# Split float32 products issued for two sums in turn, in a two-block transformer on one core

## The chip, the core and the metric

The kernel runs on one core of one Trainium2 chip. The metric is device microseconds of one execution. The kernel before took a median of 2975.62 us over three runs (2973.6 to 2980.26).

Five engines appear in the profile: PE (TensorE, the matmuls, with PEld for the weight loads that go beside them), DVE (VectorE), ACT (ScalarE), POOL (GpSimd) and SP (SyncE, which here issues nearly all DMAs).

## The reference, cut to what matters

Two different blocks, each of two layers, act on 256 tokens of 1024 features in float32.

```python
def first_block(x, ...):                    # two layers
    for l in range(2):
        mixed = concat(delta_rule_heads, gated_conv, forgetting_attention)   # from x @ w_in[l]
        x = layer_norm(ALPHA * x + (mixed * mix_scale[l]) @ w_out[l])
        y = swiglu(x, ffn_w1, ffn_w3, ffn_w2) if l == 0 else mixture_of_experts(x)   # 8 experts, 2 a token
        x = layer_norm(ALPHA * x + y)

def second_block(x, mem, ...):              # two layers
    for l in range(DEPTH):
        x = x + 0.5 * swiglu_2(rmsnorm(x, ffn1_norm[l]), ...)
        proj = rmsnorm(x, mix_norm[l]) @ w_in[l]
        # window attention, a gated linear recurrence, attention over a memory; each projected to D_MODEL
        merged = g[:, :, 0] * br_attn + g[:, :, 1] * br_lru + g[:, :, 2] * br_mem
        x = x + merged @ w_out[l]
        x = x + 0.5 * swiglu_2(rmsnorm(x, ffn2_norm[l]), ...)
    return rmsnorm(x, final_norm)
```

The sketch of the first block is shortened; the second is close to the reference's own lines. Nearly all arithmetic is in the projections, in the feed-forward layers and in the experts' three matrices (1024 x 3584 each, 8 experts).

## The kernel before, in words

**Split products.** A float32 operand is cut into two parts: `hi`, the value rounded to the type that the matmul takes in one pass (float32r), and `lo`, what is left. A product of two such operands is made of three matmuls into one PSUM sum: hi by hi, hi by the other's lo, lo by the other's hi. `mm3` (line 216) issues these three back to back. Each matmul has a weight load of its own, so that PE and PEld have the same count.

**Weights** come from DRAM as one long stream in the order of their use. `load_chunk` (line 382) issues one DMA on SP's queue for up to 2048 columns into a `raw` buffer. `run_pieces` (line 317) cuts each chunk into tiles of up to 1024 columns: ACT writes `hi` (line 199), DVE subtracts and writes `lo` (line 203). There are four buffers each for `hi` and `lo` (`NHL = 4`). A `hi` buffer comes free when PE has used it.

**projS / projG** (lines 400 to 440): features on partitions. A group of output chunks of 128 features is summed over K chunks; two neighbouring chunks share one PSUM bank of 2 x 256 columns. For each k and each chunk j of the group comes one `mm3`. The weights are the stationary operand, a chunk of 256 tokens the moving one. In a group of two or more chunks every third matmul goes on to another sum; in a group of one chunk all matmuls of the group go to the same sum. Groups of one chunk are: all but the first two chunks of each feed-forward down projection (`ffn`, line 606), the last chunks of `w_out` (line 873, from `MO = 6`) and of `w_out_2` (line 1837, from chunk 4), and all gates and branch projections of the second block's mixer (`gcol`, line 1812, and `merge`, line 1816).

**projMG** (line 448): tokens on partitions; two sums, one for each half of the tokens, in two banks, one `mm3` after the other. The mixers of the first block leave part of their projections unsplit (plain float32); those the change leaves alone.

**Experts** (`_experts`, line 1420). A block of work is one expert `e` and 512 of its 3584 hidden columns `fb`: `up` sums `moe_w1` over eight k into one bank, then `moe_w3` over eight k into another, 24 matmuls of 512 columns each. Then `Silu` of the first (ACT, tile `es`) and its product with the second (DVE, `es`). `down` transposes `es`, splits it into `hh` and `hl`, and advances two sums `py` of 512 features, again three matmuls on the one and three on the other. `down` of a block is issued behind `up` of the next. There are 56 blocks. `finish` brings an expert's two sums back to token order.

**Order of the work.** The kernel's text gives each instruction a place, but a planner sets the final order on each engine: of the instructions whose inputs and buffers it reckons ready, it takes the one that comes first in the text. The engines then keep that order. So an ACT or DVE instruction that waits for PE holds back those put behind it.

**Mixer of the second block.** Gates for `NG = 5` columns of 128 features (three branches each) come first, then for each column `merge(c)`: three branch projections (4, 4 and 8 chunks of K), and behind the first three of these one more column of gates. Tiles `gg` hold at most 18 gates.

Of the kernel before, what the change touches and what calls it, by code (L numbers as in the profile page):

```python
# [15 lines left out]
ALU = mybir.AluOpType  # L16
# [16 lines left out]
# ---------------------------------------------------------------- constants  # L33
# [56 lines left out]
# ------------------------------------------------- small parameters (layout)  # L90
# [76 lines left out]
NG = 5  # L167
# [10 lines left out]
class K:  # L178
# [17 lines left out]
    # ---- engine shorthands  # L196
# [36 lines left out]
    # ---- constants and parameters  # L233
# [12 lines left out]
    def setup(self):  # L246
        """loads of the small arrays; what is worked out from them follows in setup2"""
# [7 lines left out]
    def setup2(self):  # L255
        """one step a call: the parameters, then the constants"""
# [26 lines left out]
    def setup3(self):  # L283
        """what is worked out from them once"""
# [73 lines left out]
    def preload(self, st, pieces, m):  # L358
        """the loads of the first m chunks of what comes next"""
# [31 lines left out]
    # ---- PSUM tiles: one bank each  # L391
# [6 lines left out]
    # ---- projections, features on partitions:  out[col, tok]  # L398
# [4 lines left out]
    def projG(self, st, groups, K_, rhs, evict, korder=None, hook=None, pre=None, pin=False, whole=None):  # L403
        """groups: lists of (name, idx, col0); evict(i, n, ps[128, n, 256]) for chunks i .. i + n - 1; a step for every
        split of weights"""
# [3 lines left out]
        i0, m = 0, 0  # L409
# [35 lines left out]
    # ---- projection, tokens on partitions: out[tok, cols]  # L445
# [4 lines left out]
    def projMG(self, st, name, idx, col0, w, K_, lhs, evict, tag="mm", pin=False, whole=None):  # L450
# [3 lines left out]
        for k in range(K_):  # L454
# [9 lines left out]
            for t in range(2):  # L464
                s = slice(t * 128, t * 128 + 128)
                if whole is not None:
                    self.mm(banks[t][:, :w], whole[:, k, s], rp, k == 0, k == K_ - 1)
                    continue
                self.mm3(banks[t][:, :w], (lh[:, s], ll[:, s]), rp, start=(k == 0), stop=(k == K_ - 1))
# [4 lines left out]
    # ---- norms  # L474
    def stats(self, n, mean, late_=LATE, st=None):
        """sums over the features by token of n chunks: (bank [128, 2, 2], add(c, z[, zq]))"""
# [7 lines left out]
        def add(c, z):  # L484
            """the last two chunks go to the products alone, those before are summed up first"""
# [42 lines left out]
    def ln_finish(self, st, n, eps):  # L528
        """-> PSUM bank [128, 2, 256]: rstd, -mu*rstd on every partition"""
# [16 lines left out]
    def rms_finish(self, st, n=D, out=None):  # L546
        """-> rstd on every partition [128, 256], and by token on partitions [128, 2]"""
# [22 lines left out]
    def xhl(self, k):  # L570
        """the parts of a chunk of the input; the norm's chunks are worked out a little ahead of their use"""
# [8 lines left out]
    # ---- SwiGLU; rms: works out the rstd of the input tokens, where the input doesn't hold it yet  # L580
    def ffn(self, st, n1, n3, n2, idx, evict, rms=None, mid=None, mid2=None):
# [24 lines left out]
        groups = [[(n2, idx, 0), (n2, idx, 128)]] + [[(n2, idx, c * 128)] for c in range(2, KD)]  # L606
        rhs2 = lambda k: (h[:, k], l[:, k])
        if mid2:
            self.projS(st, groups[:-1], KF, rhs2, evict)
            mid2()  # L610
            self.projS(st, groups[-1:], KF, rhs2, lambda i, n, ps: evict(KD - 1, n, ps))
        else:
            self.projS(st, groups, KF, rhs2, evict)

    # ---- block 1: residual, then LN
# [17 lines left out]
    def ln_apply(self, z, b, gname, bname, hl=True, gain=None):  # L633
        """x = LN(z) and its parts; with gain: the parts of gain * x, and the statistics of x for the RMS norm"""
# [1337 lines left out]
```

## Time and profile before

| what | value |
|---|---|
| median of three runs | 2975.62 us (2973.6 to 2980.26) |
| profiled execution: its own span, first to last instruction | 2981.4 us |
| PE busy, share of the span, matmuls | 2920.8 us, 98%, 19525 |
| PEld busy | 2647.2 us, 89% |
| DVE busy | 2159.7 us, 72% |
| ACT busy | 1752.4 us, 59% |
| DMA, mean over the span | 223 GB/s |

The profiled execution has no other time listed than its span; it is 5.8 us over the median of the runs. Stages by time from the start: first block's mixer 0 to 258 us, feed-forward 258 to 424, second mixer 424 to 683, experts 683 to 1672, and then the second block, each of whose two layers has a feed-forward layer, the mixer and another feed-forward layer.

How to read it: a matmul's recorded duration overlaps the next one's, since matmuls are pipelined. The price of a matmul in a stream is therefore the distance from its start to the next one's start, and the busy share of PE does not tell by itself how near it is to its limit. In a row of the timeline the columns are start, duration, engine, line, operation, output and inputs, shape and count; square brackets give the idle time before it and what ended it.

### The profile page before, as it was taken

How to read it: one execution, taken by the hardware profiler on the slowest of the kernel's cores; microseconds unless marked ns; L12 is line 12 of the kernel's file. 1: busy time of each engine (PE TensorE's matmuls, PEld its weight loads, DVE VectorE, ACT ScalarE, POOL GpSimd, SP SyncE). 2: the span in 40 equal slices, each digit the busy share in tenths (PEclk: the TensorE clock that was granted, in tenths of full speed). 3: DMA queues.
4: the chain of work that ended last, by engine and by line, in shares of the span. 5: the costliest groups of instructions: out<-in, count | busy, mean ns of one | idle time of the engine just before them, and what ended most of it. 6: DMA issues, size and time to landing. Idle time of an engine off the chain costs nothing.

```text
span 2981.4 us, 48787 instructions
## 1 busy us (share of the span) xinstructions
PE 2920.8 (98%) x19525; PEld 2647.2 (89%) x19525; DVE 2159.7 (72%) x3156; ACT 1752.4 (59%) x2576; POOL 77.8 (3%) x142
## 2 busy tenths in 40 slices
PE   8999999999999999999999999999999999999998
PEld 7889997888888887788878899989999999999998
DVE  5656566559988897998989866676766665866764
ACT  4345444348787776778777744565554444664543
POOL 0100001000000000000000000100000000100000
PEclk9999999899999999999999999999999999999999
DMA  5225543229899998998999745524555555335552
GB/s 196 99 86 181 187 142 128 84 95 359 346 335 364 358 357 307 350 349 335 359 369 353 281 178 184 177 107 156 206 191 189 181 189 191 137 113 194 196 192 105
DMA packets 104205, 663.77 MB, mean 223 GB/s; under 512 B 11808, under 2 KB 17952, under 8 KB 28576
## 3 DMA queue, kind: packets, MB, share of 16 engines
q1 hardware_dynamic: 101664, 658.46, 59.7%
q8 instruction: 156, 2.56, 0.3%
q10 hardware_dynamic: 2304, 2.10, 0.2%
q14 instruction: 81, 0.66, 0.1%
HBM read 657.36 MB, written 3.15 MB: 222 GB/s over the span
## 4 chain that ended last, share of the span: by engine, by line
PE 57%; DVE 2%; ACT 1%; issue 0%; POOL 0%; POOLq 0%; DVEq 0%; ACTq 0%
PE ps_mm L214 47%; PE py L214 5%; PE ps_fx L214 2%; PE ps_sm L214 2%; DVE lo L203 1%; PE ps_fx L224 0%; PE ps_sm L224 0%; DVE aa L1769 0%; ACT hi L199 0%; DVE gi L203 0%; PE ps_st L214 0%; DVE aa L203 0%; ACT xr L200 0%; DVE y L211 0%; DVE ffab L203 0%
## 5 line engine op out<-in xcount | busy, mean ns | idle before, releaser
L203 DVE TENSOR_TENSOR lo<-raw,hi 128x1024 fp32r<-128x1024 f32 (+2 forms) x1216 | 1434.1, 1205 | 398.7 <-ACT hi L199 385.4
L199 ACT ACTIVATE hi<-raw 128x1024 fp32r<-128x1024 f32 (+2 forms) x1216 | 1246.8, 1044 | 648.8 <-PE ps_mm L214 480.9
L214 PE MATMUL ps_mm<-xh,hi 128*128 128x256 f32 x2736 | 775.7, 284 | 13.0 <-ACT hi L199 8.0
L214 PE MATMUL ps_mm<-xh,lo 128*128 128x256 f32 x2736 | 771.5, 283 | 2.3 <-DVE lo L203 2.3
L214 PE MATMUL ps_mm<-xl,hi 128*128 128x256 f32 x2736 | 771.3, 282 | 0.0
L214 PEld LDWEIGHTS ps_mm<-xh,hi 128*128 128x128 f32 x2736 | 519.4, 190 | 19.0 <-ACT hi L199 8.7
L214 PEld LDWEIGHTS ps_mm<-xh,lo 128*128 128x128 f32 x2736 | 519.1, 190 | 6.4 <-issue 3.3
L214 PEld LDWEIGHTS ps_mm<-xl,hi 128*128 128x128 f32 x2736 | 519.9, 190 | 2.8 <-issue 2.4
L214 PE MATMUL ps_mm<-lo,xgh 128*128 128x512 f32 x896 | 356.7, 398 | 0.7
L214 PE MATMUL ps_mm<-hi,xgl 128*128 128x512 f32 x896 | 350.0, 391 | 0.0
L214 PE MATMUL ps_mm<-hi,xgh 128*128 128x512 f32 x896 | 349.5, 392 | 0.0
L214 PE MATMUL ps_mm<-ffl,hi 128*128 128x256 f32 x880 | 250.2, 284 | 0.0
L214 PE MATMUL ps_mm<-ffh,hi 128*128 128x256 f32 x880 | 250.2, 284 | 0.0
L214 PE MATMUL ps_mm<-ffh,lo 128*128 128x256 f32 x880 | 250.1, 284 | 0.0
L214 PEld LDWEIGHTS ps_mm<-lo,xgh 128*128 128x128 f32 x896 | 168.4, 188 | 48.4 <-DVE lo L203 16.1
L214 PEld LDWEIGHTS ps_mm<-hi,xgh 128*128 128x128 f32 x896 | 168.5, 188 | 35.5 <-ACT hi L199 0.2
L214 PEld LDWEIGHTS ps_mm<-hi,xgl 128*128 128x128 f32 x896 | 168.7, 188 | 32.4
L214 PE MATMUL py<-lo,hh 128*128 128x512 f32 x448 | 178.5, 398 | 0.5
L214 PE MATMUL py<-hi,hl 128*128 128x512 f32 x448 | 174.8, 392 | 0.5
L214 PEld LDWEIGHTS ps_mm<-ffl,hi 128*128 128x128 f32 x880 | 170.1, 193 | 0.0
L214 PEld LDWEIGHTS ps_mm<-ffh,lo 128*128 128x128 f32 x880 | 170.0, 193 | 0.0
L214 PEld LDWEIGHTS ps_mm<-ffh,hi 128*128 128x128 f32 x880 | 170.0, 193 | 0.0
(432 smaller groups left out, 3756.9 us busy)
## 6 DMA issues: line engine op xcount, KB each, us to landing
raw<-in_sm SPq DMA_DIRECT2D x336, 1024.0 KB, 7.0
raw<-in_s SPq DMA_DIRECT2D x248, 1024.0 KB, 4.8
raw<-in_s SPq DMA_DIRECT2D x40, 512.0 KB, 3.3
raw<-in_s SPq DMA_DIRECT2D x32, 256.0 KB, 2.7
raw<-in_mem SPq DMA_DIRECT2D x5, 1024.0 KB, 4.9
kv<-kvt ACTq DMA_DIRECT2D x16, 128.0 KB, 2.3
raw<-kv SPq DMA_DIRECT2D x16, 128.0 KB, 2.7
raw<-in_s SPq DMA_DIRECT2D x2, 1005.0 KB, 6.8
```

Source lines behind the costliest of these rows:

```text
L199: return self.nc.scalar.activation(out, in_, func, scale=scale, **kw)
L203: return self.nc.vector.tensor_tensor(out=out, in0=a, in1=b, op=op)
L214: return self.nc.tensor.matmul(out, lhsT=l, rhs=r, start=start, stop=stop, skip_group_check=True, **kw)
```

## The change

- A new helper `mm3s` takes several sums and issues hi by hi for all of them, then hi by lo for all, then lo by hi for all.
- `projG` collects two chunks before it calls `mm3s`; a chunk left over goes alone. The steps that `projG` yields are kept at the same places.
- `projMG` passes both halves of the tokens to `mm3s`. Unsplit products stay as they are.
- Groups of one chunk become groups of two: the down projections, the last chunks of `w_out` (6 + 2) and `w_out_2` (4 + 2 + 2), gates and branch projections (two columns of features at a time, `NG` 4 for 5).
- Experts: the stream holds `moe_w1` and `moe_w3` of the same k side by side, and `up` advances both sums together; `down` passes both `py` sums to `mm3s`; `finish` issues `yh` for both chunks, then `yl` for both.
- Comments and docstrings are removed.

```diff
+    def mm3s(self, prods):
+        for out, lp, rp, start, stop in prods:
+            self.mm(out, lp[0], rp[0], start, False)
+        for out, lp, rp, start, stop in prods:
+            self.mm(out, lp[0], rp[1], False, False)
+        for out, lp, rp, start, stop in prods:
+            self.mm(out, lp[1], rp[0], False, stop)
...
-NG = 5
+NG = 4
...
-                    self.mm3(banks[j // 2][:, j % 2], lp, rp, start=(n == 0 and (j % 2 == 0)), stop=(n == K_ - 1))
-                    if m % (CS // 128) == 0 and (n, j) != (K_ - 1, len(g) - 1):
+                    two.append((banks[j // 2][:, j % 2], lp, rp, n == 0 and j % 2 == 0, n == K_ - 1))
+                    if len(two) < 2 and j + 1 < len(g):
+                        continue
+                    self.mm3s(two)
+                    two, before = [], m - len(two)
+                    if m // (CS // 128) > before // (CS // 128) and (n, j) != (K_ - 1, len(g) - 1):
                         yield
...
-                self.mm3(banks[t][:, :w], (lh[:, s], ll[:, s]), rp, start=(k == 0), stop=(k == K_ - 1))
+            if whole is None:
+                self.mm3s([(banks[t][:, :w], (lh[:, s], ll[:, s]), rp, k == 0, k == K_ - 1) for t, s in enumerate(toks)])
+                continue
...
-        groups = [[(n2, idx, 0), (n2, idx, 128)]] + [[(n2, idx, c * 128)] for c in range(2, KD)]
+        groups = [[(n2, idx, c * 128), (n2, idx, c * 128 + 128)] for c in range(0, KD, 2)]
...
-        groups = [[('w_out', l, c * 128) for c in range(0, MO)]] + [[('w_out', l, c * 128)] for c in range(MO, 8)]
+        groups = [[('w_out', l, c * 128) for c in range(*ab)] for ab in ((0, MO), (MO, 8))]
...
-    def up_pieces(self, e, fb, names=('moe_w1', 'moe_w3')):
-        return [(n, e, k * 128, fb * 512, 512) for n in names for k in range(KD)]
+    def up_pieces(self, e, fb):
+        return [(n, e, k * 128, fb * 512, 512) for k in range(KD) for n in ('moe_w1', 'moe_w3')]
...
-            for n in ('moe_w1', 'moe_w3'):
-                ps[n] = self.bank(shape=(512,))
-                pieces = self.up_pieces(e, fb, (n,))
-                for (_, _, r, _, _), wp in self.run_pieces('sm', pieces):
-                    k = r // 128
-                    self.mm3(ps[n], (h[:, k], lo[:, k]), wp, start=(k == 0), stop=(k == KD - 1))
+            ps = {n: self.bank(shape=(512,)) for n in ('moe_w1', 'moe_w3')}
+            two = []
+            for (n, _, r, _, _), wp in self.run_pieces('sm', self.up_pieces(e, fb)):
+                k = r // 128
+                two.append((ps[n], (h[:, k], lo[:, k]), wp, k == 0, k == KD - 1))
+                if len(two) == 2:
+                    self.mm3s(two)
+                    two = []
...
-                for i in range(2):
-                    part(i, [v[:, i * 512:i * 512 + 512] for v in w], (r % 512) // 128)
+                self.mm3s([part(i, [v[:, i * 512:i * 512 + 512] for v in w], (r % 512) // 128) for i in range(2)])
...
-                for a in range(2):
-                    for n, src in enumerate((yh, yl)):
+                for n, src in enumerate((yh, yl)):
+                    for a in range(2):
...
-        gcol = lambda c: [[(W, l, o['g'] + b * D + c * 128)] for b in range(3)]
+        gcol = lambda c: [[(W, l, o['g'] + b * D + (c + j) * 128) for j in range(2)] for b in range(3)]
...
-                self.projS('s2', [[(n, l, c * 128)]], K_, lambda k: (h_[k], l_[k]), ev)
+                self.projS('s2', [[(n, l, (c + j) * 128) for j in range(2)]], K_, lambda k: (h_[k], l_[k]), ev)
...
-        for c in range(NG):
+        for c in range(0, NG, 2):
             self.projS('s2', gcol(c), KD, self.xhl, ev_g(c))
-        for c in range(KD):
+        for c in range(0, KD, 2):
             merge(c)
             if c + NG < KD:
                 self.projS('s2', gcol(c + NG), KD, self.xhl, ev_g(c + NG))
...
-        groups = [[('w_out_2', l, c * 128) for c in range(0, 4)]] + [[('w_out_2', l, c * 128)] for c in range(4, 8)]
+        groups = [[('w_out_2', l, c * 128) for c in range(*ab)] for ab in ((0, 4), (4, 6), (6, 8))]
```

More of the change, by code (lines that the diff above doesn't have):

```diff
@@ L408, in projG @@
         it = self.run_pieces(st, pieces, pre, whole is not None)
-        i0, m = 0, 0
+        i0, m, two = 0, 0, []
         self.pin, self.free = self.lazy is not None, FREE
@@ L463, in projMG @@
                 self.pin = False
[L464 to L468, printed above, removed]
-                self.mm3(banks[t][:, :w], (lh[:, s], ll[:, s]), rp, start=(k == 0), stop=(k == K_ - 1))
+            toks = [slice(t * 128, t * 128 + 128) for t in range(2)]
+            if whole is None:
+                self.mm3s([(banks[t][:, :w], (lh[:, s], ll[:, s]), rp, k == 0, k == K_ - 1) for t, s in enumerate(toks)])
+                continue
+            for t, s in enumerate(toks):
+                self.mm(banks[t][:, :w], whole[:, k, s], rp, k == 0, k == K_ - 1)
         for t in range(2):
@@ L610, in ffn @@
             mid2()
-            self.projS(st, groups[-1:], KF, rhs2, lambda i, n, ps: evict(KD - 1, n, ps))
+            self.projS(st, groups[-1:], KF, rhs2, lambda i, n, ps: evict(KD - 2, n, ps))
         else:
@@ L1474, in up @@
             h, lo = xg[e][:2]
-            ps = {}
-            for n in ('moe_w1', 'moe_w3'):
-                ps[n] = self.bank(shape=(512,))
-                pieces = self.up_pieces(e, fb, (n,))
-                for (_, _, r, _, _), wp in self.run_pieces('sm', pieces):
-                    k = r // 128
-                    self.mm3(ps[n], (h[:, k], lo[:, k]), wp, start=(k == 0), stop=(k == KD - 1))
+            ps = {n: self.bank(shape=(512,)) for n in ('moe_w1', 'moe_w3')}
[6 more added lines that the diff above has]
+                    two = []
             s = self.ph.tile([128, 4, 128], F32, name="es", tag="es", bufs=2)
@@ L1500, in part @@
             def part(i, w, j):
-                self.mm3(st['y'][i], (hh[:, j], hl[:, j]), w, start=(fb == 0 and j == 0), stop=(end and j == 3))
+                return (st['y'][i], (hh[:, j], hl[:, j]), w, fb == 0 and j == 0, end and j == 3)
             if last:
@@ L1505, in down @@
                     for (_, _, r, _, _), w in self.run_pieces('sm', pieces):
-                        part(i, w, (r % 512) // 128)
+                        self.mm3s([part(i, w, (r % 512) // 128)])
                     finish(e, i)
@@ L1806, in ev @@
             def ev(i, n, ps):
-                gg = self.u("w", "gg")
-                self.tt(gg, ps[:, 0], R, ALU.mult)
-                self.act(gg, gg, AF.Tanh, scale=0.5, bias=self.hb["gate_bias"][l][:, i * KD + c:i * KD + c + 1])
-                gates[c, i] = gg
+                b = i // 2
+                for j in range(n):
+                    gg = self.u("w", "gg")
+                    self.tt(gg, ps[:, j], R, ALU.mult)
+                    self.act(gg, gg, AF.Tanh, scale=0.5,
+                             bias=self.hb["gate_bias"][l][:, b * KD + c + j:b * KD + c + j + 1])
+                    gates[c + j, b] = gg
             return ev
-        gcol = lambda c: [[(W, l, o['g'] + b * D + c * 128)] for b in range(3)]
+        gcol = lambda c: [[(W, l, o['g'] + b * D + (c + j) * 128) for j in range(2)] for b in range(3)]
         gh = [self.u("m", "gh", F32R) for _ in range(KD)]
@@ L1817, in merge @@
             br = (('w_attn_out_2', 4, oh, ol), ('w_mem_out_2', 4, mh, ml), ('w_lru_out_2', 8, lh, ll))
-            first = None
+            first = [None, None]
             for b, (n, K_, h_, l_) in zip((0, 2, 1), br):
-                g = gates[c, b]
                 def ev(i, n_, ps):
-                    self.stt(g, g, 1.0, ps[:, 0], ALU.add, ALU.mult)
-                self.projS('s2', [[(n, l, c * 128)]], K_, lambda k: (h_[k], l_[k]), ev)
-                if first is None:
-                    first = g
-                else:
-                    self.tt(first, first, g, ALU.add)
-            self.split(gh[c], gl[c], first, 0.5)
-        for c in range(NG):
+                    for j in range(n_):
+                        g = gates[c + j, b]
+                        self.stt(g, g, 1.0, ps[:, j], ALU.add, ALU.mult)
+                        if first[j] is None:
+                            first[j] = g
+                        else:
+                            self.tt(first[j], first[j], g, ALU.add)
+                self.projS('s2', [[(n, l, (c + j) * 128) for j in range(2)]], K_, lambda k: (h_[k], l_[k]), ev)
+            for j in range(2):
+                self.split(gh[c + j], gl[c + j], first[j], 0.5)
+        for c in range(0, NG, 2):
             self.projS('s2', gcol(c), KD, self.xhl, ev_g(c))
-        for c in range(KD):
+        for c in range(0, KD, 2):
             merge(c)
```

## The prediction, made before the changed kernel was run

> **What bounds the kernel now.** I read the page's engines first, then a table of stages, then single matmuls in the timeline, and last the waits of the experts.
>
> ```profile
> span 2981.4 us, 48787 instructions
> PE 2920.8 (98%) x19525; PEld 2647.2 (89%) x19525; DVE 2159.7 (72%) x3156; ACT 1752.4 (59%) x2576; POOL 77.8 (3%) x142
> ...
> 2180.00:2270.00 90.00, 90.00 (x774) 90.00 (x773) 65.87 (x91) 46.23 (x72) 0.00 (x0) 1.00 0.51 186
> 2276.00:2291.00 15.00, 15.00 (x127) 15.00 (x127) 7.25 (x8) 6.59 (x8) 0.00 (x0) 1.00 0.50 161
> 2292.00:2338.00 46.00, 46.00 (x386) 46.00 (x385) 27.08 (x37) 22.15 (x30) 0.00 (x0) 1.00 0.51 184
> 2028.00:2056.00 28.00, 28.00 (x243) 28.00 (x242) 15.43 (x20) 13.75 (x20) 0.00 (x0) 1.00 0.45 160
> ...
> 683.00:1160.00 477.00, 473.36 (x2147) 384.09 (x2146) 425.87 (x410) 372.71 (x411) 0.00 (x0) 1.00 0.93 353
> 1180.00:1672.00 492.00, 487.89 (x2219) 396.18 (x2219) 433.88 (x421) 381.25 (x429) 0.00 (x0) 0.99 0.93 352
> ```
>
> The stage rows give width, then busy time and count for PE, PEld, DVE, ACT and POOL, the granted clock, DMA. Outside the experts PE never stops (90.00 of 90.00, clock 1.00) while DVE works 65.87: the time is the number of matmuls times the distance between two starts. A window also counts matmuls begun just before it, about two. So one 256-column product costs 90.00 / 772 = 116.6 ns where w1 and w3 take turns (2180), 15.00 / 125 = 120.0 in a down projection's pair of chunks (2276), 46.00 / 384 = 119.8 in its single chunks (2292), 28.00 / 241 = 116.2 in the gates (2028), which are single chunks. In the experts PE is nearly full too, but DVE stands at 425.87 of 477 and the DMA engines at 0.93: three resources within 11% of each other.
>
> **The change part by part.** (a) *The order of products.* The counts that it touches are three times these:
>
> ```profile
> L214 PE MATMUL ps_mm<-xh,hi 128*128 128x256 f32 x2736 | 775.7, 284 | 13.0 <-ACT hi L199 8.0
> L214 PE MATMUL ps_mm<-lo,xgh 128*128 128x512 f32 x896 | 356.7, 398 | 0.7
> L214 PE MATMUL ps_mm<-ffl,hi 128*128 128x256 f32 x880 | 250.2, 284 | 0.0
> L214 PE MATMUL py<-lo,hh 128*128 128x512 f32 x448 | 178.5, 398 | 0.5
> ```
>
> That is 8208 and 2640 of 256 columns, 2688 and 1344 of 512, with their 14880 weight loads; none is added or removed, and each keeps its operands. Does a product cost less when the one before it went to another sum? The trace has both cases. In the experts' `up` all follow in one sum; in `down` every third goes to the other bank, and where PE's order was rearranged two go to the two banks at once. In the second block, too, some neighbours belong to different chunks:
>
> ```profile
> 1025.53 0.39 PE L214 MATMUL ps_mm<-hi,xgh 128*128 128x512 f32 x1
> ...
> 1026.21 0.39 PE L214 MATMUL ps_mm<-hi,xgh 128*128 128x512 f32 x1
> ...
> 699.64 0.39 PE L214 MATMUL py<-hi,hh 128*128 128x512 f32 x1
> ...
> 701.68 0.39 PE L214 MATMUL py<-hi,hh 128*128 128x512 f32 x1
> ...
> 1036.00 0.62 PE L214 MATMUL py<-hi,hh 128*128 128x512 f32 x2
> 1036.45 0.39 PE L214 MATMUL py<-lo,hh 128*128 128x512 f32 x1
> ...
> 1730.71 0.40 PE L214 MATMUL ps_mm<-xh,lo 128*128 128x256 f32 x2
> 1730.95 0.28 PE L214 MATMUL ps_mm<-xh,hi 128*128 128x256 f32 x1
> ```
>
> One sum throughout: 1026.21 - 1025.53 is three products, 227 ns each. A third to another bank: 701.68 - 699.64 is nine, 227 each. Two hi-by-hi products to the two banks, then back to the first: 1036.45 - 1036.00 is two, 225 each, within the rounding of the starts. Two lo products of different chunks: 0.24 / 2 = 120. And the single-sum gates run at 116.2 while the pair of the down projection runs at 120.0, the wrong way round for a chain in the sum. What goes with 116 or 120 is the moving operand: `xh` here, the down projection's `ffh` there. I therefore take 0 for the order. Its bounds: a gain at most by extending 120.0 and 116.6 (the rival below), a loss at most by taking `xh` products to the price of the others, 8208 x 3.4 ns = 28 us.
>
> The page "TensorE: Matmul & The Clock Gate" of the Trainium skill, section "Back-to-back issue gap", gives N/2.4 + 2.5 ns for a warm matmul, 109 and 216 ns here; the rows stand 7 to 11 ns above it whichever sum follows. If turns brought the stream down to that gap, the estimate by the page would be 8208 x 7.5 + 2640 x 10.8 + 4032 x 10.9, about 134 us less.
>
> (b) *Experts: both sums of `up` end together.* ACT's `Silu` of w1 moves past four weight tiles to the block's end, where DVE's product already waits.
>
> ```profile
> 1027.77 1.06 ACT L199 ACTIVATE hi<-raw 128x1024 fp32r<-128x1024 f32 x1 [0.30 <-PE ps_mm L214]
> 1030.49 0.60 ACT L200 ACTIVATE es<-ps_mm 128x512 f32<-128x512 f32 x1 [1.66 <-PE ps_mm L214]
> 1030.98 1.05 ACT L199 ACTIVATE hi<-raw 128x1024 fp32r<-128x1024 f32 x1
> ...
> 1032.07 3.50 DVE L203 TENSOR_TENSOR lo<-raw,hi 128x1024 fp32r<-128x1024 f32 x3 [1.49 <-ACT hi L199]
> 1036.20 0.69 DVE L203 TENSOR_TENSOR es<-es,ps_mm 128x512 f32<-128x512 f32 x1 [0.63 <-PE ps_mm L214]
> ...
> L200 ACT ACTIVATE es<-ps_mm 128x512 f32<-128x512 f32 x56 | 33.1, 591 | 57.3 <-PE ps_mm L214 57.3
> L203 DVE TENSOR_TENSOR es<-es,ps_mm 128x512 f32<-128x512 f32 x56 | 38.3, 684 | 20.2 <-PE ps_mm L214 20.1
> ...
> PEld ps_mm L214 <- DVE lo L203: 16.1, 53, 0.6
> ...
> PEld py L214 <- DVE lo L203: 4.0, 10, 0.5
> ```
>
> Now the splitting stops twice a block. In mid-block ACT waits 1.66 us for w1's last product; the next `hi`, queued behind, is late, so DVE waits 1.49 us, and PE in turn waits for `lo`: 16.1 + 4.0 us in all. At the end DVE waits 0.63 more. The change leaves one stop, at the end; the four tiles of `hi` and `lo` may then be full. `lo` is also needed a product later (third of six, not second). What is late next is DVE's product: behind the stop comes `Silu` (0.59 us), and behind the product the `lo` tiles of `down`. Bounds: all 20 us of PE's waiting go, or each of the 56 blocks pays the `Silu`, 56 x 0.591 = 33 us. Which it is hangs on how many tiles the planner puts ahead of `Silu`. Before, it let two `hi` tiles (those of w3's first half) pass between w1's last split and its `Silu`; with two of `down`'s four tiles ahead, PE has 12 products x 0.227 = 2.7 us of work, against 0.59 + 0.68 and one split of 1.05 + 1.2, 3.5 us less the tile already half used. That is about even, and a stop is saved, so I take 0.6 of the waiting: -12 us. The DMAs of `up` keep their number and sizes; with w1 and w3 side by side a chunk of 2048 columns serves two k instead of four. The two chunks preloaded over the branch change in the same way. Two banks instead of one are needed at the start of `up`; of three, one is free and w1's comes free with `Silu`, under the 24 products of `down` (5.4 us). `finish` only swaps four products: 0.
>
> (c) *Pairs for single chunks.* The last pair's two results are evicted together after the last product. In the second block the next projection takes early chunks first and hides it; if it didn't, it would cost what follows. It is bare before the two norms of the first block's layer 0, before routing, and at the end:
>
> ```profile
> 219.08 0.41 DVE L203 TENSOR_TENSOR sz<-sz,z 128x256 f32<-128x256 f32 x1
> 219.42 0.41 DVE L203 TENSOR_TENSOR sq<-sq,zq 128x256 f32<-128x256 f32 x1
> ...
> 220.18 0.42 DVE L211 SCALAR_TENSOR_TENSOR z<-x,ps_mm 128x256 f32<-128x256 f32 x1 [0.34 <-PE ps_mm L214]
> ...
> 222.19 0.16 DVE L207 TENSOR_SCALAR ln_m<-ps_st 128x4 f32<-128x4 f32 x1 [1.59 <-PE ps_st L214]
> ```
>
> The first two of these belong to the last chunk but one and lie under products now. Afterwards its eviction (0.42) and these two (0.34 apart) come in the 2.0 us from 220.18 to 222.19. Some overlaps the last chunk's square and sums: between 0 and 1.2 us each, I take 0.75. Four places: +3 us.
>
> (d) *Gates, merges, loads.* `NG` 4 for 5 takes three groups of 2.8 us from ahead of the first merge.
>
> ```profile
> 2023.90 0.42 DVE L203 TENSOR_TENSOR mal<-ps_fx,mah 128x256 fp32r<-128x256 f32 x1 [0.46 <-ACT mah L199]
> ...
> 2054.61 0.49 ACT L200 ACTIVATE gg<-gg,gate_bias 128x256 f32<-128x256 f32 x1
> ...
> 2057.41 0.49 ACT L200 ACTIVATE gg<-gg,gate_bias 128x256 f32<-128x256 f32 x1
> ...
> raw<-in_s SPq DMA_DIRECT2D x40, 512.0 KB, 3.3
> raw<-in_s SPq DMA_DIRECT2D x32, 256.0 KB, 2.7
> ```
>
> The gates come one chunk at a time, 2.80 us apart (24 products), so they are indeed sequential single sums. The last input of the merges is ready at 2024.3, the first merge stands at 2057; 8.4 us earlier is still covered by 25. If that cover were gone, the wait would be what is lacking. The branch loads of 256 KB pair up to 512 KB and those of 512 KB to 1 MB: fewer issues on SP's queue and fewer splits, all under a full PE, 0. In the first block's mixers the hi parts may start two products before `lo` is there; I set this to 0, since fills between latency-bound steps can fall either way by a few us.
>
> **Sum.** 0 - 12 + 3 + 0 = -9 us against this execution's 2981.4 us span. It lists no other time; it is 5.8 us above the median 2975.62, so I put the difference on the median: 2967 us. The likeliest case's own range is 2957 to 2972 (from -18 to -4).
>
> **Rivals.**
> 1. *Nothing moves.* The planner's order in the experts brings the stop at the end as much as it saves in mid-block. For: DVE is full to 89%, and what PE waits for is mostly single `lo` tiles of at most 0.6 us. Against: one stop fewer. Time: +3 - 3, 2976 us.
> 2. *Slower: the product behind `Silu`.* At the end of each of the 56 blocks ACT's `Silu` waits for PE, DVE's product waits for `Silu`, and the `lo` of `down`'s second tile stands behind it in DVE's fixed order. It decides once fewer than two tiles of `down` are split ahead. Price 33 + 3 = +36 us at full; with a third of the blocks caught, +14. For: DVE has only 51 us left in 477. Against: four buffers and the full lead. Time at the full price 3012, typically 2995 us.
> 3. *The sum's chain does cost.* If 120.0 is the price with no change of sum and 116.6 with one in three, a change each time would give 120.0 - 3 x 3.4 = 109.8 ns: 8208 x 6.8 = 56 us, 2640 x 10.2 = 27, and as much per 512-column product, 4032 x 10.2 = 41; with (c) -121 us, 2855 us. Against: the 227 ns with and without a change of bank, and the gates.
> 4. *The order makes products dearer*, as bounded in (a): `xh` products at 120 ns, +28 + 3 - 12 = +19, 2995 us. Nothing in the trace speaks for it, except that the price has two levels whose cause I infer only from the operand.
>
> **How the numbers follow.** Chances: forecast 0.42, rival 1 0.22, rival 2 0.22, rival 3 0.08, rival 4 0.06. About 0.2%, 6 us, can be told from no change. Faster: 0.37 of the forecast's 0.42 and 0.08 of rival 3, 0.45. Same: the forecast's 0.05 and 0.20 of rival 1, 0.25. Slower: rivals 2 and 4 and the rest, 0.30. The range of 8 in 10 leaves out rival 3 and rival 2 at near its full price: 2944 (all waiting of experts, 20 us, and as much again where only one engine waits) to 3004 us (-9 + 36 on the median, rounded up).
>
> **What would show it.** (a) The same windows after: 116 to 117 ns for `xh`, 120 for `ffh`, 227 in the experts; anything near 110 or 216 makes rival 3 right. (b) The row of ACT's `es` should lose most of its 57.3 us or keep it at the block's end; PE's waits for `lo` should fall from 20 to about 8; if DVE's `es` row waits for ACT by more than 20 us and PE's waits grow, rival 2 is right. (c) From the first eviction after the last product to the norm's first small operation 2.0 us before (220.18 to 222.19), about 2.8 after. (d) PE full between 2024 and the first merge. The prediction is wrong if a stage outside the experts and the four tails changes by over 5 us.

## The result, and the profile after

The changed kernel is about 1% slower: 3014.51 us in the median of four executions (2994.37 to 3016.42), against 2977.67 us of the kernel before beside it, a ratio of 1.011 with an interval of 1.0072 to 1.0149. A second comparison (e5) gave 3007.35 against 2974.20 us, 1.010 (1.0077 to 1.0122). The prediction was 2967 us, with a range from 2944 to 3004.

First the two spans with their mean granted clock. The changed kernel:

```profile
core 0: 3014.6 us, clock 0.976
```

The kernel before:

```profile
core 0: 2981.4 us, clock 0.978
```

The table of stages, for stretches with the same work in both kernels: from the last product of the first feed-forward layer to the first product of the experts (the layer-1 mixer), the first four experts, the last four; then one steady stretch of w1 and w3 and one of a down projection. The columns are those of the prediction. The kernel before:

```profile
423.00:672.20 249.20, 240.29 (x1526) 210.09 (x1525) 151.21 (x364) 111.64 (x251) 21.08 (x22) 0.90 0.29 103
672.20:1169.40 497.20, 493.56 (x2254) 400.85 (x2252) 444.02 (x440) 387.45 (x436) 0.00 (x0) 1.00 0.93 354
1211.00:1682.40 471.40, 468.61 (x2127) 379.68 (x2128) 416.68 (x399) 362.17 (x401) 0.00 (x0) 1.00 0.93 353
```

The changed kernel:

```profile
420.40:679.60 259.20, 248.64 (x1526) 217.15 (x1526) 151.70 (x367) 112.63 (x252) 20.98 (x22) 0.87 0.27 99
679.60:1192.10 512.50, 497.21 (x2254) 403.17 (x2252) 452.22 (x440) 392.48 (x435) 0.00 (x0) 1.00 0.90 343
1235.50:1710.50 475.00, 469.11 (x2128) 380.67 (x2127) 421.26 (x400) 363.26 (x402) 0.00 (x0) 1.00 0.91 350
...
2210.00:2300.00 90.00, 90.00 (x774) 90.00 (x773) 65.39 (x89) 46.12 (x72) 0.00 (x0) 1.00 0.52 188
...
2326.00:2356.00 30.00, 30.00 (x253) 30.00 (x251) 16.78 (x23) 13.44 (x18) 0.00 (x0) 1.00 0.58 200
```

The number of matmuls is the same (x2254, x1526), and outside the experts so is the price of a product: 90.00 / 772 = 116.6 ns for `xh`, 30.00 / 251 = 119.5 ns for `ffh`, as before. The experts lost time, 15.3 us in the first four and 3.6 in the last four, with the branch between them 1.8 us longer (41.6 and 43.4 us between the two rows). The layer-1 mixer is 10.0 us longer, but at a clock of 0.87 for 0.90: length times clock is 224 us before and 226 after.

Inside the experts, the lines and waits of the changed kernel that answer to the prediction's. Lines, with what ended the idle time:

```profile
L200 ACT ACTIVATE es<-ps_mm 128x512 f32<-128x512 f32 x56 | 33.5, 597 | 38.7 <-PE ps_mm L214 37.1
...
L203 DVE TENSOR_TENSOR es<-es,ps_mm 128x512 f32<-128x512 f32 x56 | 38.4, 685 | 22.3 <-ACT es L200 19.8 <-PE ps_sm L234 2.4
```

The waits in the experts (us in total, times, longest; L234 is the transposes, L224 in the kernel before):

```profile
PEld ps_mm L214 <- DVE lo L203: 16.9, 32, 0.6
...
PE ps_sm L234 <- DVE es L203: 8.0, 7, 1.2
...
PE py L214 <- ACT hh L199: 5.3, 5, 1.5
PEld py L214 <- DVE lo L203: 4.7, 8, 0.8
...
PE ps_mm L214 <- ACT es L200: 1.9, 1, 1.9
```

ACT's `es` lost 20 of its 57.3 us of waiting for PE, a third and not most of it, and the waits for `lo`, which are those of the weight loads (PEld), stayed (16.9 + 4.7 for 16.1 + 4.0). PE itself has new ones: seven times its transposes wait for DVE's product, 8.0 us, and once a product waits 1.9 us for `Silu`. Both can be seen in the timeline. The transposes, on PE, with the idle time before and its releaser in brackets:

```profile
744.06 0.62 PE L214 MATMUL ps_mm<-hi,xgl 128*128 128x512 f32 x2
744.51 0.60 PE L234 MATMUL ps_sm<-cst,es 128*128 128x128 f32 x4
746.32 0.44 PE L234 MATMUL ps_sm<-cst,es 128*128 128x128 f32 x2 [1.21 <-DVE es L203]
746.57 0.73 PE L214 MATMUL py<-hi,hh 128*128 128x512 f32 x2
...
695.14 0.39 PE L214 MATMUL ps_mm<-hi,xgh 128*128 128x512 f32 x1
697.38 0.50 PE L214 MATMUL ps_mm<-hi,xgh 128*128 128x512 f32 x1 [1.85 <-ACT es L200]
```

At 744.51 the four transposes of the block before stand at the block's end, and those of the block itself right behind them. These need `Silu` and the product, which with both sums of `up` ending together can only start now. In these first blocks the next one then has no transposes at its end, and the one after again eight. ACT's rows show the rhythm, and at 695 the second stop:

```profile
695.43 1.28 ACT L200 ACT_TABLE_LOAD   x1
696.73 0.60 ACT L200 ACTIVATE es<-ps_mm 128x512 f32<-128x512 f32 x1
...
709.06 0.60 ACT L200 ACTIVATE es<-ps_mm 128x512 f32<-128x512 f32 x1
...
728.16 0.60 ACT L200 ACTIVATE es<-ps_mm 128x512 f32<-128x512 f32 x1
...
744.48 0.60 ACT L200 ACTIVATE es<-ps_mm 128x512 f32<-128x512 f32 x1
...
1005.44 0.60 ACT L200 ACTIVATE es<-ps_mm 128x512 f32<-128x512 f32 x1 [1.43 <-PE ps_mm L214]
...
1022.68 0.60 ACT L200 ACTIVATE es<-ps_mm 128x512 f32<-128x512 f32 x1 [1.43 <-PE ps_mm L214]
```

From 709.06 to 744.48 two blocks take 35.42 us; later one takes 17.24 (1005.44 to 1022.68), two 34.48. In the kernel before a steady block takes 17.14, from this row to that at 1030.49 in the prediction:

```profile
1013.35 0.60 ACT L200 ACTIVATE es<-ps_mm 128x512 f32<-128x512 f32 x1 [1.66 <-PE ps_mm L214]
```

In the first block of all, w1's and w3's next banks are both wanted at once, one of three is free, and the second comes free only behind the loading of `Silu`'s table (1.28 us) and `Silu`: no product starts between 695.14 and 697.38, and for 1.85 us of this PE is idle.

### The profile page after: what moved, and what is told of

It reads as the page before. It is cut to its first block, busy times and chain, and to the rows that moved or that the text cites. A ratio compares the mean times of both kernels' runs of the same rounds, so it can differ in the third digit from the quotient of the medians.

```text
span 3014.6 us, 48643 instructions
## 1 busy us (share of the span) xinstructions
PE 2934.5 (97%) x19525; PEld 2656.9 (88%) x19525; DVE 2167.5 (72%) x3140; ACT 1757.3 (58%) x2560; POOL 77.3 (3%) x142
## 4 chain that ended last, share of the span: by engine, by line
PE 47%; issue 7%; DVE 4%; ACT 2%; POOL 0%; POOLq 0%; ACTq 0%; DVEq 0%
PE ps_mm L214 40%; DVE lo L203 3%; PE py L214 3%; PE ps_sm L214 2%; PE ps_fx L214 2%; ACT hi L199 1%; PE ps_fx L234 0%; DVE aa L1783 0%; PE ps_st L214 0%; DVE gi L203 0%; DVE acc L203 0%; DVE aa L203 0%; PE ps_sm L234 0%; ACT xr L200 0%; DVE es L203 0%
## 5 line engine op out<-in xcount | busy, mean ns | idle before, releaser
L214 PE MATMUL ps_mm<-xh,hi 128*128 128x256 f32 x2736 | 558.0, 284 | 12.8 <-ACT hi L199 8.1
L214 PE MATMUL ps_mm<-xl,hi 128*128 128x256 f32 x2736 | 555.8, 282 | 0.0
L214 PE MATMUL ps_mm<-xh,lo 128*128 128x256 f32 x2736 | 553.0, 282 | 1.8 <-DVE lo L203 1.8
L214 PEld LDWEIGHTS ps_mm<-xh,hi 128*128 128x128 f32 x2736 | 424.0, 190 | 19.1 <-ACT hi L199 8.6
L214 PEld LDWEIGHTS ps_mm<-xl,hi 128*128 128x128 f32 x2736 | 424.0, 190 | 3.1 <-issue 2.4
L214 PEld LDWEIGHTS ps_mm<-xh,lo 128*128 128x128 f32 x2736 | 423.1, 190 | 3.9 <-DVE lo L203 2.0
L214 PE MATMUL ps_mm<-lo,xgh 128*128 128x512 f32 x896 | 284.5, 397 | 4.7 <-DVE lo L203 2.2
L214 PEld LDWEIGHTS ps_mm<-lo,xgh 128*128 128x128 f32 x896 | 165.2, 189 | 48.6 <-DVE lo L203 16.9
L214 PE MATMUL ps_mm<-ffh,lo 128*128 128x256 f32 x880 | 178.4, 284 | 0.0
L214 PE MATMUL ps_mm<-ffh,hi 128*128 128x256 f32 x880 | 178.2, 284 | 0.0
L214 PE MATMUL py<-hi,hh 128*128 128x512 f32 x448 | 140.3, 393 | 5.3 <-ACT hh L199 5.3
```

The lines of the kernel that those rows point to most:

```text
L214: return self.nc.tensor.matmul(out, lhsT=l, rhs=r, start=start, stop=stop, skip_group_check=True, **kw)
```

## The experiments

One thing had to be settled first. Executions of one and the same kernel spread by over 1% (the kernel before: 2965.19 to 2996.50 us in 35), far above the 0.2% that I took as what can be told from no change. Each execution lists its time and its mean granted clock, and the two go together: time times clock is 2921.0 us for these 35, with a standard deviation of 1.6, and 2921.1 and 2920.3 beside the other kernels (23 and 32 executions). So I compare kernels by this product, which takes out the clock that an execution happened to get, and give the plain ratio with it. It does so only nearly: the six of the 35 at 0.984 and above average 2923.3 us, the six at 0.977 and below 2919.2. A difference of 2 or 3 us between kernels at different clocks is therefore not shown by it.

| kernel | median us | ratio to before, interval | clock | time x clock | against before |
|---|---|---|---|---|---|
| changed (first four) | 3014.51 | 1.011, 1.0072 to 1.0149 | 0.975 to 0.983 | 2942.2 | +21 |
| e5, changed again | 3007.35 | 1.010, 1.0077 to 1.0122 | 0.974 to 0.983 | 2943.9 | +22.8 |
| e1, `up` back | 2988.82 | 1.0038, 1.0018 to 1.0059 | 0.974 to 0.982 | 2930.4 | +9.4 |
| e2, `up` alone | 2988.48 | 1.0032, 1.0009 to 1.0055 | 0.979 to 0.986 | 2934.8 | +13.8 |
| e3, mixers back | 3001.57 | 1.0068, 1.0045 to 1.0092 | 0.977 to 0.986 | 2944.3 | +23.3 |
| e4, order alone | 2994.67 | 1.005, 1.0027 to 1.0074 | 0.974 to 0.980 | 2926.5 | +5.5 |
| e6, `finish` alone | 2982.38 | 1.0014, 0.9996 to 1.0032 | 0.979 to 0.986 | 2926.2 | +5.1 |
| e7, w1 leads | 2987.88 | 1.0041, 1.0021 to 1.0061 | 0.974 to 0.982 | 2924.0 | +2.9 |
| e8, early transposes | 2997.65 | 1.0075, 1.0048 to 1.0102 | 0.971 to 0.978 | 2922.7 | +1.6 |
| e9, chunks in turn only | 2998.34 | 1.008, 1.0054 to 1.0105 | 0.974 to 0.982 | 2938.5 | +18.2 |
| e10, pairs | 2984.49 | 1.0026, 1.0004 to 1.0047 | 0.977 to 0.982 | 2926.3 | +6.0 |
| e11, lead and early transposes on the kernel before | 2966.44 | 0.9946, 0.9926 to 0.9966 | 0.977 to 0.983 | 2902.7 | -17.6 |
| e12, the same with the pairs | 2965.33 | 0.9961, 0.9942 to 0.998 | 0.977 to 0.983 | 2907.6 | -12.7 |

**Which part costs: e1 to e4.**

e1, the changed kernel with `up` as before:

```diff
-            for (n, _, r, _, _), wp in self.run_pieces('sm', self.up_pieces(e, fb)):
-                two.append((ps[n], (h[:, k], lo[:, k]), wp, k == 0, k == KD - 1))
+            for n in ('moe_w1', 'moe_w3'):
+                for (_, _, r, _, _), wp in self.run_pieces('sm', self.up_pieces(e, fb, (n,))):
+                    self.mm3(ps[n], (h[:, k], lo[:, k]), wp, start=(k == 0), stop=(k == KD - 1))
```

> The changed kernel with the experts' `up` put back: w1's 24 products, then w3's; all the rest of the change stays. Theory A (the experts' order costs the time): the profiled executions put 20.6 us of the 33 us in the experts (672.2 to 1682.4 before, 679.6 to 1710.5 after), so this kernel should come to 3014.5 - 20.6 = about 2994 us, the experts should last 1010 us again, and the row of `es` products should lose its wait for ACT (19.8 us). Rival B (the whole rest is the granted clock, 0.978 before and 0.976 after, and the layer-1 mixer's 0.90 against 0.87): taking `up` back changes little, 3005 to 3016 us, and the clock stays at 0.976.

e2, the kernel before with this part of the change and no other:

> The kernel before with the experts' `up` alone changed (w1 and w3 in turn, chunk by chunk of k). Theory A: 2977.7 + 20.6 = about 2998 us, with the blocks of the first four experts 17.04 and 18.38 us long by turns for longer than before. My prediction's step (b): 2977.7 - 12 = 2966 us. Rival B: within 5 us of 2978 us at the same clock.

e3, the changed kernel, in the first block's mixers one sum after the other (`width` is 1 there and 2 elsewhere):

```diff
-                    if len(two) < 2 and j + 1 < len(g):
+                    if len(two) < self.width and j + 1 < len(g):
```

> The changed kernel with the first block's mixers (their projections up to w_out) in the old order, sum after sum; everything else as changed. Theory C (the +10 us between 420 and 680 us come from the new order of the fills in the layer-1 mixer): 3014.5 - 10 = about 3004 us. Rival B (that stage did the same work at a lower clock: 252 us x 0.90 = 227, 260 us x 0.87 = 226): the order is not the cause, the time stays at 3010 to 3016 us or goes with the clock that this stage happens to be granted.

e4, the kernel before with `mm3s` in `projG`, `projMG` and `down` and the new order in `finish`, its groups unchanged:

> The kernel before with the order of products alone: turns in every group that holds two chunks already, between token halves, in `down` and in `finish`; no new pairs, no change of `up`, of the gates or of the merges. My step (a), the order costs nothing at all: 2977.7 us within 6. Theory C: the mixers of the first block take part, so +10, about 2988 us. Rivals 3 and 4 of the prediction would give under 2930 and about 3005 us, and other prices in steady windows than 116.6 and 120 ns for a 256-column product.

Measured: `up` alone adds 13.8 us (e2). Taking it back removes 2943 - 2930.4 = 13 us (e1; 2943 is the mean of the changed kernel's two values), and DVE's product waits for PE again as before; theory A holds for three fifths of the loss, and my -12 us had the wrong sign. Putting the mixers back (e3) changes nothing, 2944.3 for 2943 (its plain median, 3001.57 us, would have fitted theory C, but its clock was higher), and the same stage of e2 shows why its length means little. In the kernel with `up` alone:

```profile
423.30:659.10 235.80, 226.88 (x1526) 198.99 (x1525) 151.24 (x364) 111.50 (x251) 21.08 (x22) 0.96 0.30 109
659.10:1169.80 510.70, 496.33 (x2254) 403.04 (x2252) 451.99 (x440) 391.37 (x436) 0.00 (x0) 1.00 0.91 344
```

The same 1526 matmuls in 235.8, 249.2 or 259.2 us at 0.96, 0.90 or 0.87: 226, 224 and 226 us at full clock. Theory C falls; the 10 us of this stage are the clock. The first four experts, at a clock of 1.00, have 13.5 of the 15.3 us with `up` alone. Most of it lies in a few blocks. From DVE's product of the sixth block to that of the thirteenth, first in the kernel with `up` alone and then in the kernel before:

```profile
760.50:896.50 136.00, 128.92 (x597) 104.86 (x598) 117.32 (x114) 104.22 (x121) 0.00 (x0) 1.00 0.86 325
```

```profile
770.90:896.80 125.90, 125.46 (x589) 103.16 (x589) 111.66 (x112) 100.47 (x120) 0.00 (x0) 1.00 0.91 341
```

These seven blocks are 10.1 us longer, and PE stands still for 7.1 us of them (136.00 - 128.92) instead of 0.4: 4.6 us in wait for `hh`, the transposed tile's `hi` part, and 2.4 for `es`. The surprise is e4: the order alone adds 5.5 us, where my step (a) had 0 and theory C 10.

**`finish`: e6, with e5 beside it.** e5 is the changed kernel again.

> The changed kernel itself, with more executions. In the four others of this study the time of every execution times its granted clock is the same within 2 us for one kernel (2921.0 us before, 2930.4, 2934.8, 2944.3, 2926.5), and the executions of one kernel differ by their clock alone (0.974 to 0.986). If so, the +36.8 us of the first comparison are about +22 of work (2942.2 - 2921.0, over 0.980) and the rest a low clock in three of four executions: the median should come to 3001 us, 2942.2 / 0.980. If the change itself lowers the clock (rival), the median stays at 3012 to 3016 us and the clock at 0.976.

e6, the kernel before with one edit:

```diff
-                for a in range(2):
-                    for n, src in enumerate((yh, yl)):
+                for n, src in enumerate((yh, yl)):
+                    for a in range(2):
```

> The kernel before with the four products of each half `finish` in the order hi, hi, lo, lo over two chunks in place of hi, lo, hi, lo; nothing else. My prediction set this to 0. The blocks at the end of an expert are 19.20 us long before and 20.02 with the order alone, the blocks between 17.15 and 17.13 to 17.17: theory D, `finish` is the part of the order that costs: 7 ends x 0.8 = +5.7 us, time times clock 2926 to 2927 us. Rival: it is `down`, or the two together: then 2921 us as before.

e6 has 2926.2, all that e4 has: `finish` is the part, and `down` costs nothing. Its lines show the way. The sums' addition in the kernel before:

```profile
L203 DVE TENSOR_TENSOR acc<-acc,ps_sm 128x512 f32<-128x512 f32 x32 | 20.5, 680 | 1.9 <-PE ps_sm L214 1.8
```

And with the new order in `finish` alone, from the same view, and from its timeline on DVE:

```profile
L203 DVE TENSOR_TENSOR acc<-acc,ps_sm 128x512 f32<-128x512 f32 x32 | 20.5, 682 | 7.1 <-PE ps_sm L214 7.1
```

```profile
1059.94 1.41 DVE L211 SCALAR_TENSOR_TENSOR yl<-py,gslot,yh 128x512 fp32r<-128x512 f32 x2
1062.10 0.69 DVE L203 TENSOR_TENSOR acc<-acc,ps_sm 128x512 f32<-128x512 f32 x1 [0.75 <-PE ps_sm L214]
```

The timeline of the kernel before at the same place:

```profile
1059.62 1.40 DVE L211 SCALAR_TENSOR_TENSOR yl<-py,gslot,yh 128x512 fp32r<-128x512 f32 x2
1060.96 1.23 DVE L203 TENSOR_TENSOR lo<-raw,hi 128x1024 fp32r<-128x1024 f32 x1
1062.11 0.68 DVE L203 TENSOR_TENSOR acc<-acc,ps_sm 128x512 f32<-128x512 f32 x1
```

The planner had put a split (`lo`, 1.23 us) between `yl` and the addition; with the four products in the other order it no longer does, and DVE, the fullest engine here but for PE, waits 0.75 us for PE instead. The idle time grew by 5.2 us, time times clock by 5.1.

The changed kernel again (e5) kept its product, 2943.9 for 2942.2, at a clock of 0.979 in the median; the median time is 6 us above the 3001 that I had expected. 22.8 / 0.980 = 23 us of its loss are thus there at any clock. Whether the change also lowers the clock a little (0.979 against 0.982 of the kernel before beside it) I can't tell: single executions of both reach from 0.974 to 0.983 and more.

**Where in `up`: e7, e8 and e9.** e7 lets w1 run ahead, on the changed kernel:

```diff
-        return [(n, e, k * 128, fb * 512, 512) for k in range(KD) for n in ('moe_w1', 'moe_w3')]
+        p = {n: [(n, e, k * 128, fb * 512, 512) for k in range(KD)] for n in ('moe_w1', 'moe_w3')}
+        a, b = p['moe_w1'], p['moe_w3']
+        return a[:4] + [q for two in zip(a[4:], b[:4]) for q in two] + b[4:]
```

> The changed kernel with the experts' w1 four chunks of k ahead of w3: w1's first four alone, then four products of k of both in turn, then w3's last four. Silu can then run two weight tiles before the block's end. Theory E (what costs is that both sums end together, at the block's end, where Silu, product, transposes and the free bank are then waited for in a row): most of the 13 us of `up` goes, time times clock about 2942.2 - 10 = 2932 us, and the first expert's stop of 2.24 us for a free bank goes. Rival F (the turns themselves cost, wherever the sums end): half the products still take turns, so at least half the 13 us stays, 2936 us or more.

e8 moves the head of `down`, on the changed kernel:

```diff
-        def down(e, fb, s):
+        def turn(e, fb, s):
             pt = self.bank("sm", shape=(4, 128))
...
+            return e, fb, hh, hl
...
                     self.mm3s(two)
                     two = []
+                    if k == 3:
+                        mid()
```

where `mid` calls `turn` for the block before.

> The changed kernel with the transposes of the block before, and their hi and lo parts, issued after the fourth chunk of k of the next block's `up`, and no longer at the head of `down`. Theory G (the extra time of the first four experts is the alternation of 17.04 and 18.38 us, in which the transposes of two blocks stand together at a block's end): the blocks become 17.1 to 17.25 us from the first one on; 13 x 0.5 = 6 us less in the first half and up to 2 in the second, time times clock 2934 us. Rival (the alternation comes from Silu at the block's end, wherever the transposes stand): 2940 us or more, still with blocks of 18.4.

e9 keeps the weights in turn, and each chunk's three products together, on the changed kernel:

```diff
-                if len(two) == 2:
-                    self.mm3s(two)
-                    two = []
+                self.mm3s(two)
+                two = []
```

> The changed kernel with the experts' weights in turn (w1's and w3's chunk of each k side by side) but each chunk's three products together again, so that two of three products follow in one sum. Theory E (both sums ending together costs, not the turns): time times clock stays at the changed kernel's 2943 us, within 3. Rival F (the turns of the products cost): it falls to 2930 us, that of the kernel with `up` put back.

By time times clock either of the first two moves takes away 19 to 20 us, about the whole loss and more than I had expected: 2924.0 and 2922.7 for 2943. By plain time e8 is not shown to be as good: its median, 2997.65 us, is 10 us under the changed kernel's beside it (e5), but its six executions had the lowest clock of all kernels (0.971 to 0.978), and whether the edit itself lowers the clock stays open. What the edit does to the experts is seen at a clock of 1.00, in their first four and last four:

```profile
673.20:1172.70 499.50, 494.74 (x2253) 403.08 (x2252) 447.25 (x440) 387.02 (x435) 0.00 (x0) 1.00 0.92 352
1214.00:1686.00 472.00, 468.49 (x2128) 380.93 (x2127) 421.00 (x401) 362.28 (x403) 0.00 (x0) 1.00 0.93 354
```

That is 13.0 and 3.0 us less than in the changed kernel. With w1 leading, the steady blocks are shorter than in either kernel:

```profile
1008.33 0.60 ACT L200 ACTIVATE es<-ps_mm 128x512 f32<-128x512 f32 x1 [1.43 <-PE ps_mm L214]
...
1025.15 0.60 ACT L200 ACTIVATE es<-ps_mm 128x512 f32<-128x512 f32 x1 [1.43 <-PE ps_mm L214]
```

16.82 us from one `Silu` to the next, where the changed kernel has 17.24; the stop for a bank in the first block is gone too, while e8 keeps it (1.8 us). With the transposes early the rhythm of 35.42 us for two blocks is gone from the first block on, as its rows show:

```profile
703.15 0.60 ACT L200 ACTIVATE es<-ps_mm 128x512 f32<-128x512 f32 x1
...
736.79 0.60 ACT L200 ACTIVATE es<-ps_mm 128x512 f32<-128x512 f32 x1
```

That is 33.64 us for two. Its `Silu` and product still stand at the block's end, and DVE's product even waits longer for ACT:

```profile
L203 DVE TENSOR_TENSOR es<-es,ps_mm 128x512 f32<-128x512 f32 x56 | 38.3, 684 | 23.9 <-ACT es L200 23.7
```

So that wait costs little by itself: what costs is that PE's transposes, and the splits of their result, stand behind it. With both moved to mid-block no transpose and no hi-by-hi product of `down` waits for DVE or ACT in e8. Theory G holds. The new order of the weights in the stream is not the cause, since e8 keeps it. With e9 the answer is mixed: 2938.5, so the sums ending together keep most of the 13 us (theory E). The 5 us that it gains cannot be put down to the products' turns alone, because with three products together w1's sum also ends two products (0.45 us) earlier: DVE's product then waits at most 0.9 us for `Silu`, where in the changed kernel it is 1.4. Its first four experts:

```profile
670.90:1176.70 505.80, 494.33 (x2253) 401.93 (x2252) 450.65 (x440) 388.73 (x435) 0.00 (x0) 1.00 0.91 348
```

505.8 us, between 512.5 and 497.2; the last four are as in the changed kernel.

**The pairs, and a version that is faster: e10 to e12.** e10 is e1 with `finish` put back as well.

> The changed kernel with `up` and `finish` put back: what is left are the pairs for single chunks, the gates and merges in pairs, and the turns outside the experts. My steps (a), (c) and (d) gave 0 + 3 + 0 us: time times clock 2921.0 + 3 = 2924 us. From the runs so far, 2930.4 (with `up` back) - 5.2 (`finish`) = 2925 us, and the experts as long as before within 1 us.

It stands 6.0 us above the kernel before, 3 more than my steps gave. Its experts are as before:

```profile
677.90:1175.40 497.50, 493.88 (x2253) 400.71 (x2252) 444.23 (x440) 387.19 (x435) 0.00 (x0) 1.00 0.92 354
```

e11 is the kernel before with the edits of e7 and e8 in the experts, e12 the changed kernel with both and `finish` back:

> The kernel before with two moves in the experts alone: w1 leads w3 by four chunks of k (the middle four of both in turn), and the transposes of the block before are issued after w1's fourth chunk. Neither pairs nor `finish` nor the rest of the change. If what each move gave on the changed kernel adds (blocks of 16.8 us in place of 17.15, no alternation of 17.3 and 18.1), some 45 blocks lose 0.35 to 0.9 us: time times clock 2900 to 2906 us, against 2921.0. If the two moves give the same gain (rival), about 2913 us.

> The changed kernel with w1 leading by four chunks, the early transposes and `finish` put back: the pairs and the turns stay. By the pairs' price of 3 to 4 us it should stand that much above the kernel before with the same two moves, 2904 to 2910 us of time times clock; if the pairs gain something once the experts don't stop, below it.

The two moves together give more than either alone: e12 is 16.4 us under e7 and 15.1 under e8, of which `finish` accounts for about 5. On the kernel before (e11) they give 2902.7, 17.6 us under it, and by the plain medians 2966.44 against 2980.84 us. The first four and last four experts of e11:

```profile
673.00:1161.90 488.90, 487.82 (x2254) 402.70 (x2252) 442.22 (x440) 386.45 (x436) 0.00 (x0) 1.00 0.94 360
1203.50:1666.10 462.60, 462.18 (x2128) 381.96 (x2127) 416.05 (x402) 362.24 (x402) 0.00 (x0) 1.00 0.94 360
```

PE now stands still for only 1.1 and 0.4 us of these stretches (488.90 - 487.82), against 3.6 and 2.8 before; the rest of the gain was in products that stood further apart than 227 ns, which the records count as busy (493.56 against 487.82 us). A steady block in which `Silu`s follow 16.82 us apart is 72 products of 227 ns, 16.3 us, and four transposes, so that there PE has almost nothing left to give. The weight loads' waits for `lo` in the experts went from 16.1 + 4.2 us to 1.6 + 3.3. The pairs cost 4.9 us on top (e12).

## Why the prediction was wrong

**(a) The order of products: right on the price, wrong on the 0.** 116.6 and 119.5 ns stayed, and so did the 512 columns (744.06 to 744.51, two products in 0.45 us), so rival 3 (2855 us) and rival 4 (products dearer) fall. `down` is free, and so are the mixers (e3, e4 less e6); the 5 us of the order are those of `finish`, below. The Trainium skill gives in "TensorE: Matmul & The Clock Gate", section "Back-to-back issue gap", N/2.4 + 2.5 ns for an isolated matmul at the full clock, by estimate 109 ns at 256 columns. The stretches measured here do not come down to it, whichever sum follows.

**(b) The experts: the step that failed.** I wrote that one stop is saved, and took 0.6 of what I read as PE's 20 us of waiting for `lo` as gain, -12 us. It measured +13 to +14. The 20 us are waits of the weight loads (PEld); PE itself stood still for only 3.6 + 2.8 us of the kernel before's two stretches. They did not go with the stop in mid-block: they are 16.9 + 4.7 us after. They go when w1 leads (6.3 + 6.6 us in e7) and not when the transposes are early (22.5 + 1.7 in e8). And I costed the end of the block by what is queued on ACT and DVE (`Silu`, product, `lo` of `down`), and not by who reads the product: the transposes on PE, which the planner puts, in the first experts, at the end of every second block, right behind the last product of `up`. The kernel before has the same rhythm in its first blocks and the same 35.4 us for two of them (`Silu` at 711.01 and 746.42 us); there the wait is for `hh`, 5.5 us in all. What costs is that the changed kernel stays in it longer (PE waits seven times for `es` and five times for `hh`, 8.0 + 5.3 us, where before it was 0.3 + 5.5). It also pays 0.1 us more in each steady block (17.24 for 17.14) and has the stop for a bank. For the banks I wrote that w1's comes free under the 24 products of `down`; the first block has no `down` before it.

**`finish`, "only swaps four products: 0": wrong by 5 us.** I looked at PE, where four products cost the same in any order. The edit moved a split on DVE.

**(c) Pairs: right in kind.** The tail before the first norm of the first block, on DVE:

```profile
216.65 0.75 DVE L211 SCALAR_TENSOR_TENSOR z<-x,ps_mm 128x256 f32<-128x256 f32 x2 [1.16 <-PE ps_mm L214]
...
219.78 0.16 DVE L207 TENSOR_SCALAR ln_m<-ps_st 128x4 f32<-128x4 f32 x1 [1.70 <-PE ps_st L214]
```

3.1 us from the eviction to the norm's first operation, for 2.0 before: +1.1, near the upper bound of 1.2 and not 0.75; of the four tails this is the one that was measured. With all pairs and turns outside the experts that came to 4 to 6 us (e1 less e6, e12 less e11, e10) for my +3. (d) The mixers of the first block are 0, as I had set them, within what e3 can tell (1 us), and the cover in the second block's mixer held: PE is busy 35.90 of the 36.00 us from 2020.

**The rivals and the sum.** In outcome it was rival 2's (2995 to 3012 us), and its sign, a `es` row waiting for ACT by about 20 us and more waiting on PE, came true (19.8). Its first half, DVE's product behind `Silu`, is what the rows show. Its second half falls: it had the product hold up the `lo` of `down`, and e8 keeps the wait for `Silu` and is rid of the loss. The parts add up: 13.8 (`up`) + 5.1 (`finish`) + 4 to 6 (pairs) = 23 to 25 us for 22.8 measured. Two figures of the prediction do not follow from its own terms, without bearing on this: +14 us for rival 2 gives 2990 and not 2995, and 20 us twice gives a lower bound of 2936 and not 2944. What was not in the prediction at all is the clock: it moved medians of the same kernel by more than the 6 us that I called measurable. My last condition, a stage outside the experts changing by over 5 us, was met by the layer-1 mixer, and it was the clock.

What stays open is why the planner leaves the rhythm of eight transposes later in the first four experts of the changed kernel than before. Its reasons are not in a trace, and e9 does not separate the turns from the earlier end of w1's sum.

## What to carry to other kernels

When two sums are made to end together, look at who reads the result of the two and where that reader stands in its own engine's order: the cost was not in the products, nor in the wait of the next engine, but in the transposes that had nothing between them and the end of the sums. Let one sum lead, and give the reader's work a place in the middle of the next block. And compare kernels by time times granted clock when executions differ by their clock: 5 us could be told here within a spread of 30.

## What the hardware showed that I had not expected

Time times mean granted clock is nearly constant for a kernel: 35 executions from 2965.19 us at 0.986 to 2996.50 us at 0.975 give 2921.0 us, with a deviation of 1.6. In the profiled executions the clock stands at a half in some stretches, and how long these are differs from one to the next. Two places of the changed kernel, in the table of stages:

```profile
524.00:554.70 30.70, 30.70 (x127) 28.09 (x127) 11.13 (x24) 7.97 (x23) 1.78 (x2) 0.50 0.08 28
...
698.00:701.50 3.50, 3.50 (x10) 2.73 (x9) 3.45 (x4) 2.69 (x4) 0.00 (x0) 0.51 0.82 281
701.50:705.00 3.50, 3.50 (x16) 2.87 (x16) 2.50 (x3) 2.81 (x4) 0.00 (x0) 1.00 0.81 330
```

After the stop at 695, in which PE is idle for 1.85 us, the clock is at a half for 3.4 us (3.50 us at a mean of 0.51): 10 products, where the next 3.50 us hold 16. And in the layer-1 mixer it stays at a half for 30.7 us, although PE is listed as busy throughout; it is a stretch of small products (x127), and the kernel before has 20.5 us of the same there:

```profile
523.20:543.70 20.50, 20.50 (x85) 18.71 (x83) 8.10 (x18) 3.95 (x10) 1.64 (x1) 0.50 0.00 1
```

The Trainium skill has the clock's window in "TensorE: Matmul & The Clock Gate", section "Part 1: The HAM clock gate (the "warmup" mystery)": 3413 ns, free-running, and a half clock after an idle window. The length agrees: the stretches of 3.4, 30.7 and 20.5 us are 1, 9 and 6 times 3.41 us. That a whole idle window is needed does not agree: 1.85 us of idle time were enough after 695, and the two long stretches list no idle time at all. The ends of the matmuls are modelled, so how idle PE was inside the long stretches the trace cannot tell.
